# Taps of a causal depthwise convolution: from diagonal float32r products to float32 products of four taps by 32 channels in four column tiles

## The chip, the cores and the metric

The kernel runs as one launch on one core of a Trainium2 chip. The metric is device time in microseconds of that core. A core has TensorE for matrix products (PE in the profile; PEld is its loading of the stationary operand), VectorE (DVE), ScalarE (ACT), GpSimd (POOL) and SyncE (SP). SP here issues every data transfer and computes nothing. PSUM is the memory that TensorE writes, SBUF the working memory of 128 partitions.

## The reference, cut to what matters

The program is two transformer blocks on 512 tokens of width 1024, all in float32. The change lies in one mixer of the second block, a Conformer convolution:

```python
def causal_dwconv(x, w):
    k_w = w.shape[0]
    return lax.conv_general_dilated(
        x, w[:, None, :].astype(x.dtype), window_strides=(1,), padding=[(k_w - 1, 0)],
        dimension_numbers=('NWC', 'WIO', 'NWC'), feature_group_count=x.shape[-1])

def conformer_conv(h, w_in, b_in, dw, dw_b, ln_g, ln_b, w_out, b_out):
    D = h.shape[-1]
    u = h @ w_in + b_in
    u = u[..., :D] * jax.nn.sigmoid(u[..., D:])
    u = causal_dwconv(u, dw) + dw_b
    u = jax.nn.silu(layernorm(u, ln_g, ln_b))
    return u @ w_out + b_out
```

Each of the 1024 channels is convolved over time with its own 31 taps (CONV_WIDTH = 31). There is no product across channels in the taps.

## The kernel before, in words

Data lie with channels on partitions: a tensor of 1024 channels is eight tiles of 128 partitions by 512 tokens, the groups m = 0 to 7. Nearly the whole program is dense matrix products. To keep float32 precision they are split: a value is written as hi + lo in the faster type float32r, and `mm3` (L357 to L361) does three products, hi by lo, lo by hi and hi by hi, on lines 359, 360 and 361. `weights` (L311 to L326) loads a weight block of 128 x 2048 into `raw` by SP (L322), casts it to `whi` on ACT (L323) and subtracts on VectorE, or on the engine `lo_on`, to get `wlo` (L324).

The stage is `conformer`. Its loop has three steps per group:

- `inputs(m)` loads the weights of the group and makes two products of 24 float32r matmuls each, for the gate and the value. The low part of the weights is made on VectorE for groups 0 and 1 and on GpSimd for the rest. Three buffers of whi and wlo take turns; `raw` has two.
- `gated(m)` makes u = (value + bias) * sigmoid(gate + bias) (L1176 sg, L1177 the sigmoid, L1181 t, L1183 u) into one of three padded buffers `ub` with 30 zeros ahead of the 512 tokens. Then it puts some taps on TensorE: u is split into uh (ACT, L1187) and ul (GpSimd, L1188), and for each of these taps ACT writes two 128 x 128 diagonal matrices with the tap's rates (L1193, dgh and dgl), and `mm3` multiplies them with u shifted by the tap. Groups 0 to 4 have 5 such taps, then 6, 10 and 20: 61 in all. ACT brings the sum to SBUF with the bias (L1196).
- `convolved(m)` does the rest. VectorE multiplies and adds one tap after the other (L1204 the first, then L1218, `scalar_tensor_tensor`, 128 x 512), alternating between two accumulators. For groups 0 to 6 six further taps are multiplied on ACT (L1211) and added on GpSimd (L1213). GpSimd adds the parts (L1220, L1222); for group 7 VectorE does (L1224, L1225).
- `summed(m)` subtracts an approximate mean on GpSimd (L1234; the mean comes from group 0 alone, L1232), squares on ACT (L1236) and adds both to running sums over channels by two float32 products with a matrix of 1/1024 (L1238).

The loop is software-pipelined: in turn m come inputs(m + 1), gated(m), summed(m - 2), convolved(m - 1). The order on each engine's queue is fixed when the program is built: a list scheduler simulates the engines and takes the instructions that are ready, the earlier of the program first. Every queue runs in order, SP's too.

After the loop the variance is made from the sums (L1253 to L1255), then the norm, SiLU and the output product follow; these lines do not change.

Elsewhere in the program, the attention of the first block has float32 products whose stationary operand is 64 columns wide and whose output is one half of the 128 PSUM partitions: single ones in `stick_breaking` (L727), and pairs for two heads, issued one behind the other into both halves, in `pair` (L776). The linear-recurrence stage copies between SBUF tiles by SP (L1585, ME<-AR, 64 partitions).

Of the kernel before, what the change touches and what calls it, by code (L numbers as in the profile page):

```python
# [11 lines left out]
F32 = mybir.dt.float32  # L12
F32R = mybir.dt.float32r
# [6 lines left out]
P = 128  # L20
# [65 lines left out]
def host(inp):  # L86
# [64 lines left out]
    vec("conv_dw", b["conv_dw"][0].reshape(31, KT, P).transpose(2, 1, 0).reshape(P, 248))  # L151
# [984 lines left out]
def conformer(k):  # L1136
    nc, tc, c = k.nc, k.tc, k.c
    W, PE_TAPS, POOL_TAPS = 31, (5,) * 5 + (6, 10, 20), (6,) * 7 + (0,)
    with ExitStack() as s1:
        k.psum(s1, 6)  # L1140
        stp = k.pool(s1, name="cf_st", bufs=1, space=PSUM)
# [4 lines left out]
        sums = [stp.tile([P, S], F32, name=f"sum{i}") for i in range(2)]  # L1146
        with ExitStack() as s2:
# [3 lines left out]
            ub = [tp.tile([P, S + W - 1], F32, name=f"ub{i}", bufs=1) for i in range(3)]  # L1151
            for u in ub:
                nc.gpsimd.memset(u[:, 0:W - 1], 0.0)  # L1153
            d = lambda m, j: k.v("conv_dw", m * W + j)
            rate_h = tp.tile([P, KT * W], F32R, name="rate_h", bufs=1)
            rate_l = tp.tile([P, KT * W], F32, name="rate_l", bufs=1)
            o0, _ = k.at["conv_dw"]
            raw = k.vecs[:, o0:o0 + KT * W]
            nc.scalar.copy(rate_h, raw)
            nc.gpsimd.tensor_tensor(rate_l, raw, rate_h.bitcast(F32), op=ALU.subtract)  # L1160
            rates = rate_h.bitcast(F32), rate_l

            def inputs(m):
# [3 lines left out]
                w = k.weights(k.I["conv_in"][m], 256, lo_on=nc.gpsimd if m > 1 else None)  # L1167
# [5 lines left out]
            def gated(m, ps, psv):  # L1173

                sg = tp.tile([P, S], F32, name="sg_t")
# [7 lines left out]
                nc.vector.scalar_tensor_tensor(u[:, W - 1:], t, k.v("conv_b_in", m), sg, op0=ALU.add, op1=ALU.mult)  # L1183
                ps = k.mm.tile([P, S], F32, name="ps")
                n = PE_TAPS[m]
# [9 lines left out]
                if m < KT - 1:  # L1195
                    nc.scalar.activation(conv[m], ps, AF.Identity, bias=k.v("conv_dw_b", m))  # L1196
                return u, ps

            def convolved(m, u, ps):

                o = conv[m]
                n = PE_TAPS[m]
                o2 = tp.tile([P, S], F32, name="conv2")
                nc.vector.tensor_scalar(o2, u[:, n:n + S], d(m, n), None, op0=ALU.mult)  # L1204
                if m == KT - 1:
                    n += 1
                    nc.vector.tensor_scalar(o, u[:, n:n + S], d(m, n), k.v("conv_dw_b", m), op0=ALU.mult, op1=ALU.add)
                o3 = None
                for j in range(W - POOL_TAPS[m], W):
                    t = tp.tile([P, S], F32, name="ct" if o3 else "conv3")  # L1210
                    nc.scalar.activation(t, u[:, j:j + S], AF.Copy, scale=d(m, j))  # L1211
                    if o3:
                        nc.gpsimd.tensor_tensor(o3, o3, t, op=ALU.add)  # L1213
                    else:
                        o3 = t
# [705 lines left out]
```

## Time and profile before

| what | value |
|---|---|
| time, median of 3 runs | 2643.24 us (2641.21 to 2645.35) |
| the profiled execution: time | 2642.88 us |
| its span, first to last instruction | 2641.1 us |
| mean granted TensorE clock | 0.969 |
| busy share of the span | PE 94%, PEld 75%, DVE 62%, ACT 44%, POOL 15% |
| transfers | 249.59 MB, mean 95 GB/s |

The profile is of one execution. Times in it are microseconds from the start of the span, and durations of groups are busy time, mean ns of one. A row of a group names line, engine, operation and tiles as out<-in; what follows the bar is busy time and mean, then the idle time of the engine just before, with what ended it. In the timeline equal instructions that follow each other are merged into one row with their count. Matmuls overlap, and their recorded ends are modelled, so TensorE is better read from start to start. The granted clock is a share of full speed: 1.00 is 2.4 GHz and 0.50 is 1.2 GHz.

### The profile page before, as it was taken

How to read it: one execution, taken by the hardware profiler on the slowest of the kernel's cores; microseconds unless marked ns; L12 is line 12 of the kernel's file. 1: busy time of each engine (PE TensorE's matmuls, PEld its weight loads, DVE VectorE, ACT ScalarE, POOL GpSimd, SP SyncE). 2: the span in 40 equal slices, each digit the busy share in tenths (PEclk: the TensorE clock that was granted, in tenths of full speed). 3: DMA queues.
4: the chain of work that ended last, by engine and by line, in shares of the span. 5: the costliest groups of instructions: out<-in, count | busy, mean ns of one | idle time of the engine just before them, and what ended most of it. 6: DMA issues, size and time to landing. Idle time of an engine off the chain costs nothing.

```text
span 2641.1 us, 32709 instructions
## 1 busy us (share of the span) xinstructions
PE 2471.1 (94%) x13005; PEld 1992.1 (75%) x13005; DVE 1628.8 (62%) x2217; ACT 1161.9 (44%) x1934; POOL 383.3 (15%) x291
## 2 busy tenths in 40 slices
PE   7999999999997999999998999999966798999997
PEld 6777777888886777878777888888744587888886
DVE  5345665543346877776466474646899665665655
ACT  5464544332234455665545342424534543433333
POOL 1001000000002663332010000000576300000000
PEclk9999999999998999999999999999988899999999
DMA  5113334222223544121332222222210031222221
GB/s 171 61 52 103 120 120 158 80 96 98 99 84 125 180 164 146 63 57 49 122 110 80 80 96 96 96 96 81 95 48 16 16 128 49 96 96 96 96 92 68
DMA packets 72837, 249.59 MB, mean 95 GB/s; under 512 B 8296, under 2 KB 19688, under 8 KB 54888
## 3 DMA queue, kind: packets, MB, share of 16 engines
q1 hardware_dynamic: 72684, 247.50, 27.5%
q8 instruction: 102, 1.67, 0.3%
q14 instruction: 51, 0.42, 0.0%
HBM read 217.84 MB, written 25.43 MB: 92 GB/s over the span
## 4 chain that ended last, share of the span: by engine, by line
PE 80%; DVE 12%; ACT 3%; DMA 3%; issue 2%; POOL 1%; SPq 0%; DVEq 0%; ACTq 0%; POOLq 0%
PE ps L359 19%; PE ps L360 19%; PE ps L361 19%; DVE conv L1218 5%; PE pt L1606 3%; PE fl L359 1%; PE fl L360 1%; PE fl L361 1%; PE y L1707 1%; DVE wlo L324 1%; PE pt L1583 1%; ACT whi L323 1%; PE y L1706 1%; PE o L776 1%; PE s L703 1%
## 5 line engine op out<-in xcount | busy, mean ns | idle before, releaser
L323 ACT CAST whi<-raw 128x2048 fp32r<-128x2048 f32 (+4 forms) x251 | 346.1, 1386 | 537.2 <-PE ps L361 439.1
L324 DVE TENSOR_TENSOR wlo<-raw,whi 128x2048 fp32r<-128x2048 f32 (+4 forms) x232 | 384.4, 1661 | 198.2 <-ACT whi L323 194.2
L930 DVE TENSOR_TENSOR x<-ps,x 128x512 f32<-128x512 f32 x94 | 64.1, 690 | 218.8 <-PE ps L361 218.8
L1218 DVE SCALAR_TENSOR_TENSOR conv<-ub,vecs,conv 128x512 f32<-128x512 f32 x136 | 162.5, 1250 | 0.4
L324 POOL TENSOR_TENSOR wlo<-raw,whi 128x2048 fp32r<-128x2048 f32 (+2 forms) x19 | 60.9, 3209 | 632.5 <-ACT whi L323 632.5
L1120 ACT ACTIVATE cv<-u,vecs 128x512 f32<-128x512 f32 x88 | 63.0, 720 | 150.3 <-DVE u L1118 150.1
L1118 DVE TENSOR_TENSOR u<-ps,rms 128x512 f32<-128x512 f32 x88 | 60.3, 688 | 76.1 <-PE ps L361 76.0
L1345 POOL TENSOR_SCALAR mx<-h,vecs 128x512 f32<-128x512 f32 x40 | 80.5, 2017 | 61.5 <-DVE mx6l L351 25.8
L1618 ACT CAST qb<-pt 128x512 bf16<-128x512 f32 x112 | 63.8, 590 | 37.2 <-PE pt L1606 36.3
L1289 POOL TENSOR_TENSOR fo<-x,rms 128x256 f32<-128x256 f32 x6 | 4.9, 843 | 486.1 <-DVE rms L415 486.1
L1121 DVE SCALAR_TENSOR_TENSOR cv<-u,vecs,cv 128x512 f32<-128x512 f32 x88 | 65.7, 748 | 11.2 <-ACT cv L1120 10.9
L359 PE MATMUL ps<-xg0h,wlo 128*128 128x512 f32 x164 | 68.8, 421 | 2.7 <-ACT xg0h L353 1.9
L360 PE MATMUL ps<-xg0l,whi 128*128 128x512 f32 x164 | 65.0, 397 | 3.6 <-DVE xg0l L354 3.6
L1153 POOL MEMSET ub<- 128x30 f32 x3 | 0.3, 123 | 461.5 <-DVE cv L1122 461.5
L1122 DVE SCALAR_TENSOR_TENSOR cv<-u,vecs,cv 128x512 f32<-128x512 f32 x88 | 65.8, 749 | 1.7
L359 PE MATMUL ps<-xg1h,wlo 128*128 128x512 f32 x164 | 65.7, 401 | 0.0
L360 PE MATMUL ps<-xg1l,whi 128*128 128x512 f32 x164 | 65.7, 400 | 0.0
L1625 DVE CAST_PREDICATED Z<-ball,pt 128x512 bf16<-128x512 int16 x80 | 53.1, 683 | 20.2 <-PE pt L1606 19.7
L360 PE MATMUL ps<-xg7l,whi 128*128 128x512 f32 x164 | 64.1, 391 | 1.4 <-DVE xg7l L354 1.4
L361 PE MATMUL ps<-xg1h,whi 128*128 128x512 f32 x164 | 64.9, 396 | 0.0
L361 PE MATMUL ps<-xg0h,whi 128*128 128x512 f32 x164 | 64.7, 394 | 0.0
L359 PE MATMUL ps<-xg2h,wlo 128*128 128x512 f32 x164 | 64.7, 395 | 0.0
(1253 smaller groups left out, 7562.5 us busy)
## 6 DMA issues: line engine op xcount, KB each, us to landing
raw<-ffn_in SPq DMA_DIRECT2D x44, 1024.0 KB, 4.7
raw<-xkv SPq DMA_DIRECT2D x64, 256.0 KB, 2.9
raw<-w_up SPq DMA_DIRECT2D x16, 1024.0 KB, 4.8
raw<-w_down SPq DMA_DIRECT2D x16, 1024.0 KB, 4.8
raw<-ffn_out SPq DMA_DIRECT2D x16, 1024.0 KB, 4.8
rk_scr<-ev SPq DMA_DIRECT2D x48, 256.0 KB, 2.4
raw<-w_in_fm SPq DMA_DIRECT2D x16, 512.0 KB, 4.6
pg<-rk_scr SPq DMA_DIRECT2D x8, 1024.0 KB, 5.7
```

Source lines behind the costliest of these rows:

```text
L323: a = hi_on.tensor_copy(hi[:, m], raw) if hi_on else nc.scalar.copy(hi[:, m], raw)
L324: b = (lo_on or nc.vector).tensor_tensor(lo[:, m], raw, hi[:, m].bitcast(F32), op=ALU.subtract)
L359: nc.tensor.matmul(ps, wl, xh, start=start, stop=False, skip_group_check=skip)
L360: nc.tensor.matmul(ps, wh, xl, start=False, stop=False, skip_group_check=skip)
L361: nc.tensor.matmul(ps, wh, xh, start=False, stop=stop, skip_group_check=skip)
L930: nc.vector.tensor_tensor(k.x[i], ps, k.x[i], op=ALU.add)
L1121: nc.vector.scalar_tensor_tensor(t, u[:, 1:S + 1], d(1), t, op0=ALU.mult, op1=ALU.add)
L1122: nc.vector.scalar_tensor_tensor(t, u[:, 0:S], d(0), t, op0=ALU.mult, op1=ALU.add)
L1218: nc.vector.scalar_tensor_tensor(a, u[:, j:j + S], d(m, j), a, op0=ALU.mult, op1=ALU.add)
L1345: nc.gpsimd.tensor_scalar(t, h[m][:, 0:S], k.v(f"mu{i}", m), None, op0=ALU.mult)
L1606: nc.tensor.matmul(o[:, u], lhs[:, u] if len(lhs.shape) == 3 else lhs, rhs[:, u] if len(rhs.shape) == 3 else rhs, start=True, stop=True)
L1618: nc.scalar.copy(t, o)
```

## The change

The taps 0 to 19 go to TensorE for every group, the other 11 stay with one ACT and ten VectorE operations. For the products, the 128 channels of a group are cut into four blocks g of 32. A tile `ut` of 128 partitions holds, for block g, four copies of its 32 channels one under the other, copy j shifted by j tokens; sixteen transfers by SP make it from u. A block `dg[:, 4s + g]` of 128 x 32 holds at row 32j + i, column i the rate of tap 4s + j of channel i of block g. One float32 product of dg with `ut[:, g]` from token 4s on then adds four taps for 32 channels, and its output is 32 of the 128 PSUM partitions. Five steps s by four blocks g are 20 products a group. dg is made by one VectorE multiplication of a mask with rates from a new input, `conv_taps`, that also carries all the taps and is loaded by one transfer at the start of the stage; the taps leave the common vector table. The low parts of all weights are made on VectorE. The two accumulators become one, the last addition reads PSUM. The running sums become additions on VectorE, with two products after the loop instead of two in each turn.

```diff
+CONV_STEPS = 5
...
+    dw = b["conv_dw"][0]
+    pk = dw[:4 * CONV_STEPS].reshape(CONV_STEPS, 4, KT, 4, 32).transpose(1, 4, 2, 0, 3).reshape(P, -1)
+    a["conv_taps"] = np.concatenate([dw.reshape(31, KT, P).transpose(2, 1, 0).reshape(P, 248), pk,
+                                     np.arange(P)[:, None] % 32 == np.arange(32)[None]], 1)
...
-    W, PE_TAPS, POOL_TAPS = 31, (5,) * 5 + (6, 10, 20), (6,) * 7 + (0,)
+    W, NS = 31, CONV_STEPS
+    L = S + W + 1
...
-        k.psum(s1, 6)
-        stp = k.pool(s1, name="cf_st", bufs=1, space=PSUM)
+        k.psum(s1, 8)
...
+        taps = cp.tile([P, 248 + KT * NS * 4 + 32], F32, name="taps")
+        nc.sync.dma_start(taps, k.I["conv_taps"])
...
-                w = k.weights(k.I["conv_in"][m], 256, lo_on=nc.gpsimd if m > 1 else None)
+                w = k.weights(k.I["conv_in"][m], 256)
...
+                dg = tp.tile([P, NS * 4, 32], F32, name="dg")
+                nc.vector.tensor_tensor(dg, mask.unsqueeze(1).to_broadcast([P, NS * 4, 32]),
+                                        rows[:, m].unsqueeze(2).to_broadcast([P, NS * 4, 32]), op=ALU.mult)
...
-                uh, ul = [tp.tile([P, S + W - 1], F32R, name=nm) for nm in ("uh", "ul")]
-                nc.scalar.copy(uh, u)
-                nc.gpsimd.tensor_tensor(ul, u, uh.bitcast(F32), op=ALU.subtract)
-                for j in range(n):
-                    dg = []
-                    for nm, r in zip(("dgh", "dgl"), rates):
-                        dg.append(tp.tile([P, P], F32R, name=nm, bufs=6))
-                        nc.scalar.activation(dg[-1], c["ident"], AF.Copy, scale=r[:, m * W + j:m * W + j + 1])
-                    k.mm3(ps, *dg, uh[:, j:j + S], ul[:, j:j + S], j == 0, j == n - 1)
+                ut = tp.tile([P, 4, L - 4], F32, name="ut")
+                for j in range(4):
+                    for g in range(4):
+                        nc.sync.dma_start(ut[32 * j:32 * j + 32, g], u[32 * g:32 * g + 32, j:j + L - 4])
+                return u, ut, dg
...
+                for s in range(NS):
+                    for g in range(4):
+                        nc.tensor.matmul(ps[32 * g:32 * g + 32], dg[:, 4 * s + g], ut[:, g, 4 * s:4 * s + S],
+                                         start=s == 0, stop=s == NS - 1, skip_group_check=True)
+                o, n = conv[m], 4 * NS
+                nc.scalar.activation(o, u[:, n:n + S], AF.Identity, scale=rate(m, n), bias=k.v("conv_dw_b", m))
+                for j in range(n + 1, W):
+                    nc.vector.scalar_tensor_tensor(o, u[:, j:j + S], rate(m, j), o, op0=ALU.mult, op1=ALU.add)
+                nc.vector.tensor_tensor(o, ps, o, op=ALU.add)
...
-                nc.gpsimd.tensor_tensor(o, o, mean, op=ALU.subtract)
-                q = tp.tile([P, S], F32, name="csq")
+                nc.vector.tensor_tensor(o, o, mean, op=ALU.subtract)
+                q = tp.tile([P, S], F32, name="csq") if m else total[1]
                 nc.scalar.activation(q, o, AF.Square)
-                for i, r in enumerate((o, q)):
-                    nc.tensor.matmul(sums[i], c["ones_d"], r, start=(m == 0), stop=(m == KT - 1))
+                if m:
+                    nc.vector.tensor_tensor(total[0], conv[0] if m == 1 else total[0], o, op=ALU.add)
+                    nc.vector.tensor_tensor(total[1], total[1], q, op=ALU.add)
...
+            sums = [k.mm.tile([P, S], F32, name="ps") for _ in range(2)]
+            for ps, r in zip(sums, total):
+                nc.tensor.matmul(ps, c["ones_d"], r, start=True, stop=True)
```

## Rows read from the trace of the kernel before

**Rows 1.** The page, part 4: the chain that ended last, by line.

```profile
PE ps L359 19%; PE ps L360 19%; PE ps L361 19%; DVE conv L1218 5%; PE pt L1606 3%; PE fl L359 1%; PE fl L360 1%; PE fl L361 1%; PE y L1707 1%; DVE wlo L324 1%; PE pt L1583 1%; ACT whi L323 1%; PE y L1706 1%; PE o L776 1%; PE s L703 1%
```

**Rows 2.** Busy time by stretch: start of the stage, loop, tail, one input set.

```profile
core 0: us, PE busy (x) PEld busy (x) DVE busy (x) ACT busy (x) POOL busy (x), PEclk, DMA share, GB/s
1858.70:1881.00 22.30, 21.35 (x92) 16.94 (x92) 14.76 (x11) 11.42 (x12) 9.53 (x2) 1.00 0.38 132
1881.00:2070.00 189.00, 137.54 (x506) 102.02 (x504) 187.98 (x169) 90.27 (x188) 125.01 (x66) 0.86 0.10 36
2070.00:2091.00 21.00, 6.44 (x8) 2.51 (x8) 8.64 (x7) 7.54 (x11) 15.34 (x12) 0.64 0.00 0
1900.70:1911.60 10.90, 10.90 (x49) 8.82 (x47) 10.90 (x12) 6.04 (x10) 6.15 (x5) 1.00 0.00 0
```

**Rows 3.** Groups of VectorE in the stage: busy us, mean ns.

```profile
L1218 DVE SCALAR_TENSOR_TENSOR conv<-ub,vecs,conv 128x512 f32<-128x512 f32 x136 | 162.5, 1250 | 0.4
L1204 DVE TENSOR_SCALAR conv<-ub,vecs 128x512 f32<-128x512 f32 x8 | 9.0, 1123 | 0.7 <-POOL conv L1220 0.6
L1183 DVE SCALAR_TENSOR_TENSOR ub<-t,vecs,sg_t 128x512 f32<-128x512 f32 x8 | 7.0, 871 | 0.0
L324 DVE TENSOR_TENSOR wlo<-raw,whi 128x2048 fp32r<-128x2048 f32 x3 | 6.8, 2283 | 0.7 <-ACT whi L323 0.7
L1176 DVE TENSOR_TENSOR sg_t<-ps,rms 128x512 f32<-128x512 f32 x8 | 5.4, 680 | 0.0
L1181 DVE TENSOR_TENSOR t<-ps,rms 128x512 f32<-128x512 f32 x8 | 5.4, 678 | 0.0
...
L1225 DVE TENSOR_TENSOR conv<-ps,conv 128x512 f32<-128x512 f32 x1 | 0.7, 692 | 0.0
```

**Rows 4.** L1218: min/median/max ns; then its timeline where GpSimd idles.

```profile
L1218 DVE SCALAR_TENSOR_TENSOR conv<-ub,vecs,conv x136: 735/745/5105, 1881.6 to 2069.1; 128x512 f32<-128x512 f32 x136
...
2061.71 6.05 DVE L1218 SCALAR_TENSOR_TENSOR conv<-ub,vecs,conv 128x512 f32<-128x512 f32 x9
```

**Rows 5.** Groups of GpSimd in the stage, the first two of six.

```profile
L1213 POOL TENSOR_TENSOR conv<-conv,ct 128x512 f32<-128x512 f32 x35 | 57.1, 1634 | 22.1 <-ACT ct L1211 20.6 <-ACT conv L1211 0.8
L324 POOL TENSOR_TENSOR wlo<-raw,whi 128x2048 fp32r<-128x2048 f32 x6 | 29.7, 4943 | 34.6 <-ACT whi L323 34.6
```

**Rows 6.** Timeline of TensorE: the first product of the stage.

```profile
1858.76 0.39 PE L359 MATMUL ps<-xg0h,wlo 128*128 128x512 f32 x1
```

**Rows 7.** Timeline of all engines behind the last taps.

```profile
2069.74 0.69 DVE L1225 TENSOR_TENSOR conv<-ps,conv 128x512 f32<-128x512 f32 x1
2069.89 1.26 POOL L1220 TENSOR_TENSOR conv<-conv,conv 128x512 f32<-128x512 f32 x1 [11.03 <-DVE conv L1218]
...
2073.89 2.08 PE L1238 MATMUL sum<-conv,call 128*128 128x512 f32 x2 [4.18 <-POOL conv L1234]
...
2079.41 0.60 ACT L1253 ACTIVATE var<-sum 128x512 f32<-128x512 f32 x1 [3.69 <-PE sum L1238]
```

**Rows 8.** Groups of ACT in the stage.

```profile
L323 ACT CAST whi<-raw 128x2048 fp32r<-128x2048 f32 x9 | 17.0, 1898 | 8.1 <-PE ps L361 8.1
L1177 ACT ACTIVATE sg_t<-sg_t,vecs 128x512 f32<-128x512 f32 x8 | 5.8, 723 | 36.8 <-DVE sg_t L1176 36.8
...
L1211 ACT ACTIVATE conv<-ub,vecs 128x512 f32<-128x512 f32 x7 | 5.1, 722 | 11.8 <-POOL conv L1222 11.8
L1236 ACT ACTIVATE csq<-conv 128x512 f32<-128x512 f32 x8 | 5.0, 627 | 13.5 <-POOL conv L1234 13.5
```

**Rows 9.** Timeline of TensorE: one float32 product of 512 columns, and the next.

```profile
313.53 1.02 PE L819 MATMUL s<-ka,qa 66*128 66x512 f32 x2
314.39 0.22 PE L820 MATMUL s<-ball,b_ident 128*128 128x128 bf16 x1
```

**Rows 10.** Timeline of TensorE: one 64-column product, a pair, and what follows each.

```profile
77.46 1.07 PE L727 MATMUL o<-sb_a,V 128*64 128x512 f32 x2
78.46 0.59 PE L703 MATMUL s<-sq,sk 64*128 64x384 f32 x1
...
283.19 1.08 PE L776 MATMUL o<-pts,V 128*64 128x512 f32 x4
284.20 0.59 PE L819 MATMUL s<-ka,qa 66*128 66x384 f32 x1
```

**Rows 11.** SP's queue: issue in ns (min/median/max) and landing in us, copies and loads.

```profile
L1585 SPq DMA_DIRECT2D ME<-AR x32: 461/588/675, 990.2 to 1234.6; - x32
...
DMA to landing us min/median/max: 2.2/2.3/6.5
...
L322 SPq DMA_DIRECT2D raw<-conv_in x8: 327/328/328, 1842.3 to 1915.8; - x8
...
raw<-conv_in SPq DMA_DIRECT2D x8, 1024.0 KB, 4.7
```

More of the change, by code (lines that the diff above doesn't have):

```diff
@@ L150, in host @@
     vec("conv_b_in", fm(b["conv_b_in"][0]))
-    vec("conv_dw", b["conv_dw"][0].reshape(31, KT, P).transpose(2, 1, 0).reshape(P, 248))
+    dw = b["conv_dw"][0]
+    pk = dw[:4 * CONV_STEPS].reshape(CONV_STEPS, 4, KT, 4, 32).transpose(1, 4, 2, 0, 3).reshape(P, -1)
+    a["conv_taps"] = np.concatenate([dw.reshape(31, KT, P).transpose(2, 1, 0).reshape(P, 248), pk,
+                                     np.arange(P)[:, None] % 32 == np.arange(32)[None]], 1)
     for n in ("conv_dw_b", "conv_ln_g", "conv_ln_b", "conv_b_out"):
@@ L1145, in conformer @@
         mean = cp.tile([P, S], F32, name="mean")
-        sums = [stp.tile([P, S], F32, name=f"sum{i}") for i in range(2)]
+        total = [cp.tile([P, S], F32, name=f"total{i}") for i in range(2)]
+        taps = cp.tile([P, 248 + KT * NS * 4 + 32], F32, name="taps")
+        nc.sync.dma_start(taps, k.I["conv_taps"])
+        rate = lambda m, j: taps[:, m * W + j:m * W + j + 1]
+        rows = taps[:, 248:248 + KT * NS * 4].rearrange("p (m n) -> p m n", n=NS * 4)
+        mask = taps[:, 248 + KT * NS * 4:]
         with ExitStack() as s2:
@@ L1150, in conformer @@
             rstd = None
-            ub = [tp.tile([P, S + W - 1], F32, name=f"ub{i}", bufs=1) for i in range(3)]
+            ub = [tp.tile([P, L], F32, name=f"ub{i}", bufs=1) for i in range(3)]
             for u in ub:
                 nc.gpsimd.memset(u[:, 0:W - 1], 0.0)
[L1154 to L1161, printed above, removed]
+                nc.gpsimd.memset(u[:, S + W - 1:], 0.0)
             def inputs(m):
@@ L1182, in gated @@
                 u = ub[m % 3]
-                nc.vector.scalar_tensor_tensor(u[:, W - 1:], t, k.v("conv_b_in", m), sg, op0=ALU.add, op1=ALU.mult)
-                ps = k.mm.tile([P, S], F32, name="ps")
-                n = PE_TAPS[m]
-                uh, ul = [tp.tile([P, S + W - 1], F32R, name=nm) for nm in ("uh", "ul")]
-                nc.scalar.copy(uh, u)
-                nc.gpsimd.tensor_tensor(ul, u, uh.bitcast(F32), op=ALU.subtract)
-                for j in range(n):
-                    dg = []
-                    for nm, r in zip(("dgh", "dgl"), rates):
-                        dg.append(tp.tile([P, P], F32R, name=nm, bufs=6))
-                        nc.scalar.activation(dg[-1], c["ident"], AF.Copy, scale=r[:, m * W + j:m * W + j + 1])
-                    k.mm3(ps, *dg, uh[:, j:j + S], ul[:, j:j + S], j == 0, j == n - 1)
@@ L1195, in gated @@
[L1195 to L1215, printed above, removed]
-                for j in range(n + 1, W - POOL_TAPS[m]):
-                    a = (o2, o)[(j - n) % 2]
-                    nc.vector.scalar_tensor_tensor(a, u[:, j:j + S], d(m, j), a, op0=ALU.mult, op1=ALU.add)
-                if m < KT - 1:
-                    nc.gpsimd.tensor_tensor(o, o, o2, op=ALU.add)
-                    if o3:
-                        nc.gpsimd.tensor_tensor(o, o, o3, op=ALU.add)
-                else:
-                    nc.vector.tensor_tensor(o, o, o2, op=ALU.add)
-                    nc.vector.tensor_tensor(o, ps, o, op=ALU.add)
@@ new lines, in gated, with convolved @@
+                nc.vector.scalar_tensor_tensor(u[:, W - 1:S + W - 1], t, k.v("conv_b_in", m), sg, op0=ALU.add, op1=ALU.mult)
+                ut = tp.tile([P, 4, L - 4], F32, name="ut")
[3 more added lines that the diff above has]
+                return u, ut, dg
+            def convolved(m, u, ut, dg):
+                ps = k.mm.tile([P, S], F32, name="ps")
+                for s in range(NS):
[7 more added lines that the diff above has]
+                nc.vector.tensor_tensor(o, ps, o, op=ALU.add)
```

## Prediction

> **What bounds the kernel now.** I began with the page: TensorE is the end of the chain of waits nearly everywhere, and the one line of another engine with a large share is the vector multiply-add of the convolution, L1218, at 5% [rows 1]. So the stage of the change is not bound like the rest. The table by stretch says so: in 1881 to 2070 us VectorE is busy 187.98 of 189.00 us, TensorE only 137.54 [rows 2], while in the stretch just before TensorE hardly stops. VectorE's groups show why: 136 multiply-adds take 162.5 us, a mean of 1250 ns [rows 3]. The same instruction runs at (6.05 - 0.74) / 8 = 0.66 us from start to start in a stretch where GpSimd is idle [rows 4]; GpSimd's groups (L1213, L324 and four more, each of which reads SBUF) fill 125.01 us of the stretch [rows 2, 5]. I read the slow ones as VectorE held up by GpSimd; both the count and the price of the multiply-adds are then open to the change. The stage runs from its first product at 1858.76 [rows 6] to ACT's read of the sums at 2079.41 [rows 7]: 220.6 us. A group of 128 channels costs VectorE (162.5 + 9.0 + 7.0 + 5.4 + 5.4) / 8 = 23.7 us [rows 3].
>
> **Removed.** 56 of 136 multiply-adds; on TensorE 61 taps of three float32r products; on ACT the diagonals, casts and tap products; all of GpSimd's work in the loop; eight pairs of sums. None of it but the vector work and the closing chain was on the path.
>
> **VectorE after, per group.** Ten multiply-adds 9 x 0.66 + 0.74 = 6.7 [rows 4]; the split of the weights, which moves here from GpSimd for groups 2 to 7, 2.28; sg and t 0.68 each, the last add from PSUM 0.69 [rows 3]; u 0.74, as the same operation undisturbed [rows 4]; the subtraction of the mean and two running totals, 3 x 0.68 by the t row. The diagonal block dg, 128x640 with both inputs broadcast, has no row: between t (512 elements, 0.68) and the split (2048, 2.28), by length 0.81. Sum 14.6 us, provided that GpSimd stays idle; if not, the ten would cost up to 1.7 us each. ACT has the cast 1.90, sigmoid 0.72, one tap 0.72 and square 0.63 [rows 8], 4.0 us, hidden.
>
> **TensorE after, per group.** 48 input products take 10.9 us (the last stretch of [rows 2]). The taps are five rounds of four float32 products of 128 rows by 32 columns, each round over four column tiles. A float32 product of 512 columns costs 314.39 - 313.53 = 0.86 us [rows 9]. Whether four overlap is the question of this change, and the kernel before already answers half of it: one product on a 64-column tile occupies TensorE from 77.46 to 78.46, and a pair on two such tiles with different moving data from 283.19 to 284.20 [rows 10]. The second tile is free. I extend this to four, as it is the nearest row: 5 x 0.86 plus 0.15 for entering and leaving (1.01 - 0.86) = 4.45 us. The upper end is no overlap, 20 x 0.86 = 17.2; below 4.3 nothing is possible, as one tile has five products in a row. Sum 15.35 us a group: TensorE becomes the bound, 0.75 us ahead of VectorE.
>
> **The copies.** Sixteen a group on SP's queue, SBUF to SBUF. The nearest row, ME<-AR, takes 0.59 us to issue and lands 2.3 us after issue; a weight load lands in 4.7 and takes 0.33 to issue [rows 11]. Bounds: 16 x 0.33 + 2.3 = 7.6 and 16 x 0.59 + 2.3 = 11.7 us from u to the last copy. I take 11.7, by the SBUF row. In the middle of the loop two input sets and two tap sets (2 x 10.9 + 2 x 4.45 = 30.7 us) lie between a group's input set and its own taps; u takes some 3 to 10 of them, so the copies are hidden. For the last group it is not. What waits behind the copies on SP is the next weight load: a rival below. The load of the taps is one more transfer on that queue, off the path unless its SBUF is freed late; 0 to 4.7 us, I take 0.
>
> **Sum.** TensorE starts at 1858.8, with 1 us lost at the start as before (21.35 of 22.30 us busy [rows 2]). Eight input sets are 87.2, and seven tap sets 31.2: 1978.2. The last u: input set 7 ends at 1969.3 (five tap sets ahead of it), VectorE's add for group 5 waits for its taps until 1973.7, then sg, sigmoid and u 2.1 [rows 3, 8], the copies: 1987.5. The last tap set is 4.45 at full clock, 8.9 at half; TensorE has then been idle 9 us, and the granted clock was 0.64 in the idle tail before [rows 2], so I take 6.5: 1994. Then add 0.69, subtract 0.68, square 0.63, total 0.68 and one product of about 2 us [rows 7]: 1998.7, against 2079.4. This replaces the tail of 9.7 us in which three GpSimd operations and four double products followed the last add [rows 7]. Gain 80.7 us. Against it I set 8 us for waits between two engines 0.75 us apart: none at best, one split of 2.28 late in each group, 18 us, at worst. Net 72.7: 2642.88 - 72.7 = 2570 us for the profiled execution, which is 0.36 us under the median of the runs; I forecast **2570**. Its own range: 2556 (no waits, short copies, full clock) to 2583 (18 us of waits, half clock).
>
> **Rivals.** (B) *Column tiles overlap only in part*, two at a time: a set is 10 x 0.86 + 0.15 = 8.75 us, input and tap sets end at 2017, the last u's copies delay that to 2022.4, and the sums come at 2027.4: 2591. For it: no row shows four tiles. Against: in the pair the second tile costs 10 ns (1.07 and 1.08 us [rows 10]), no sign of a shared limit.
> The Trainium skill, "TensorE: Matmul & The Clock Gate", section "Part 3: Packing small matmuls", reports 2.38 times for three column tiles and 3.07 times for four row tiles, where full overlap would be 3 and 4; by 3.07 a set would be an estimated 17.2 / 3.07 = 5.6 us and the time some 9 us above my forecast, and the pair in the trace agrees with overlap but not with a loss.
>
> (C) *Column tiles do not overlap in this order.* Each product is two records, and if TensorE starts the next tile only after the second, a set is 17.2 us; all sets end at 1859.8 + 87.2 + 137.6 = 2084.6, the copies are hidden, the sums come at 2089.6, 10 us later than now: 2653, **slower**. It decides from a set of 15.9 us up. The pair speaks against it.
>
> (D) *SP's queue.* Copies wait in order for u, and the load for the group after next may stand behind them. Its weights are then ready u + 9.4 + 4.7 + 1.9 + 2.28 = 18.3 us after u, 20.4 after the input set, and needed after 10.9 + 2 x 4.45 = 19.8; behind ten multiply-adds 6.7 later. Late by 0.6 to 7.3 us in five groups: 4 us each, 2590, at most 2607. For it: program order has the load behind the copies. Against: the loads of before were issued as soon as their buffer was free, ahead of other work.
>
> **How the numbers follow.** Forecast 0.66, B 0.12, D 0.11, C 0.11. About 0.2% (5 us) can be told from no change; C's price is twice that, so a little of it may read as the same: faster 0.88, same 0.02, slower 0.10. The range starts under the forecast's own low end, 2555, and reaches past B and D to 2612, which leaves out C and little else.
>
> **What would show it.** Right: in the profile after, multiply-adds with a mean near 0.74 us, 80 of them; GpSimd without work in the loop; the four tiles' first records a few ns apart and a tap set in about 4.5 us; TensorE dense through the loop at clock 1.00 with one gap before the last set; the sums some 73 us earlier. Wrong: tap sets of 9 or 17 us (B, C); input products that wait for wlo while SP holds copies (D); multiply-adds that stay at 1.2 us with GpSimd idle, which would break my reading of VectorE and add up to 5 us a group.

## The result and the profile after

| kernel | median | runs | ratio to before, 95% interval |
|---|---|---|---|
| before, on the same chip | 2644.3 us | 2641.21 to 2646.2 | |
| after | 2564.01 us | 2561.08 to 2567.13 | 0.9698 [0.9681, 0.9714] |

The change is faster by 80 us, 3.0%. The forecast was 2570 us in a range of 2555 to 2612. The profiled execution of after took 2561.08 us, with a span of 2558.9 us. Line numbers below are those of the changed kernel: L366 to L368 are the three products of `mm3`, L329, L330 and L331 the load of a weight block, its cast and its low part, L1195 the copies, L1203 the tap products, L1208 the multiply-adds, L1209 the addition that reads PSUM, L1241 the read of the sums.

The chain that ended last, by line, the same line of the page as in [rows 1]. The multiply-add, 5% before, is gone from it, and the tap products stand there with 1%:

```profile
PE ps L366 21%; PE ps L367 21%; PE ps L368 20%; PE pt L1594 3%; PE ps L1203 1%; DVE wlo L331 1%; PE y L1695 1%; PE fl L366 1%; DMA raw<-xkv 1%; PE fl L367 1%; ACT whi L330 1%; PE fl L368 1%; PE pt L1571 1%; PE y L1694 1%; PE o L783 1%
```

Busy time by stretch, to be read beside [rows 2]: the start of the stage, the loop, the tail, one turn of the loop, then the gap ahead of the last tap set and that set.

```profile
core 0: us, PE busy (x) PEld busy (x) DVE busy (x) ACT busy (x) POOL busy (x), PEclk, DMA share, GB/s
1855.20:1881.00 25.80, 25.80 (x113) 21.02 (x112) 19.83 (x23) 14.99 (x14) 0.00 (x0) 1.00 0.46 156
1881.00:1970.00 89.00, 89.00 (x474) 56.88 (x474) 80.34 (x109) 20.87 (x23) 0.00 (x0) 1.00 0.49 139
1970.00:1997.60 27.60, 18.90 (x129) 7.49 (x127) 19.45 (x27) 5.07 (x7) 0.00 (x0) 0.87 0.33 88
1909.00:1924.54 15.54, 15.54 (x92) 10.13 (x88) 15.35 (x22) 5.20 (x7) 0.00 (x0) 1.00 0.68 215
...
1979.60:1986.10 6.50, 0.12 (x4) 0.00 (x0) 6.50 (x11) 0.63 (x1) 0.00 (x0) 0.80 0.61 149
1986.10:1993.30 7.20, 7.12 (x40) 3.81 (x40) 1.52 (x3) 0.00 (x0) 0.00 (x0) 0.70 0.09 23
```

The bound has changed hands. In the loop TensorE is busy for all of 89.00 us at clock 1.00, VectorE for 80.34, GpSimd for nothing; before, VectorE filled 187.98 of 189.00 us.

VectorE's groups in the stage, beside [rows 3]:

```profile
L1208 DVE SCALAR_TENSOR_TENSOR conv<-ub,taps,conv 128x512 f32<-128x512 f32 x80 | 58.4, 747 | 2.6 <-ACT conv L1206 1.8
...
L1181 DVE TENSOR_TENSOR dg<-taps 128x640 f32<-128x640 f32 x8 | 6.5, 818 | 1.0 <-DMA taps<-conv_taps 1.0
...
L1209 DVE TENSOR_TENSOR conv<-ps,conv 128x512 f32<-128x512 f32 x8 | 5.5, 687 | 9.2 <-PE ps L1203 9.1
```

136 multiply-adds of 1250 ns have become 80 of 747 ns. VectorE now waits for TensorE's taps, 9.1 us in all (last row): 6.0 of them for the last set, 3.1 for the first.

The timeline of after: the stage's first product, the first tap set, one tap set between two input sets, and the end of the stage on TensorE, its weight loading (PEld), VectorE, SP and ACT, beside [rows 6, 7].

```profile
1855.21 0.39 PE L366 MATMUL ps<-xg0h,wlo 128*128 128x512 f32 x1
...
1888.85 1.04 PE L1203 MATMUL ps<-ut,dg 128*32 128x512 f32 x2
1889.82 0.50 PE L366 MATMUL ps<-xg0h,wlo 128*128 128x512 f32 x1
...
1893.76 4.48 PE L1203 MATMUL ps<-ut,dg 128*32 128x512 f32 x34
...
1907.83 1.02 PE L1216 MATMUL ps<-conv,call 128*128 128x512 f32 x2
...
1924.31 4.50 PE L1203 MATMUL ps<-ut,dg 128*32 128x512 f32 x40
1928.74 0.50 PE L366 MATMUL ps<-xg0h,wlo 128*128 128x512 f32 x1
...
1970.93 8.79 PE L1203 MATMUL ps<-ut,dg 128*32 128x512 f32 x80
...
1971.04 0.69 DVE L1189 TENSOR_TENSOR t<-ps,rms 128x512 f32<-128x512 f32 x1 [0.45 <-PE ps L368]
1971.82 0.75 DVE L1191 SCALAR_TENSOR_TENSOR ub<-t,vecs,sg_t 128x512 f32<-128x512 f32 x1
...
1975.29 0.33 SPq L329 DMA_DIRECT2D raw<-conv_out  x1
1975.72 10.81 SPq L1195 DMA_DIRECT2D ut<-ub  x16
...
1986.18 7.45 PE L1203 MATMUL ps<-ut,dg 128*32 128x512 f32 x40 [6.46 <-DVE conv L1208]
...
1987.35 0.18 PEld L1203 LDWEIGHTS ps<-ut,dg 128*32 128x32 f32 x2 [0.35 <-DMA ut<-ub]
...
1993.67 0.69 DVE L1209 TENSOR_TENSOR conv<-ps,conv 128x512 f32<-128x512 f32 x1 [5.99 <-PE ps L1203]
...
1997.04 0.60 ACT L1241 ACTIVATE var<-ps 128x512 f32<-128x512 f32 x1 [1.22 <-PE ps L1237]
```

A product is two records, so a set of 20 is x40. From start to start a tap set takes 1928.74 - 1924.31 = 4.43 us. At the end of the loop the sets of groups 5 and 6 run back to back (x80), then TensorE has nothing until the last set at 1986.18. The row names VectorE as what it waited for, but that multiply-add is no input of the products; the last copies are, and they were issued until 1986.5 (1975.72 + 10.81). The set's first products, one of each block, started one by one as the copies of their block landed, the fourth 1.8 us after the first (the PEld row shows the third waiting for a copy).

The first turn is longer than the others, 19.9 us from set 0 at 1888.85 to set 1 at 1908.78. Two things fill most of the extra 4.4 us: input products stand between the first tap products of set 0, three of which so ran alone, 0.97 us each (1889.82 - 1888.85), and the product for the mean of group 0 (L1216) takes 0.95 us.

From the first product to ACT's read of the sums the stage takes 1997.04 - 1855.21 = 141.8 us, against 220.6 before: 78.8 us of the gain. What follows it is as long as before to within 0.6 us (2561.08 - 1997.04 = 564.0; 2642.88 - 2079.41 = 563.5). This stage began 3.55 us earlier than before, but that is no gain of the change: in the traces of the runs below, none of which touches an earlier stage, it begins anywhere between 1854.5 and 1863.1. The length of the stage is steadier than the time of the run: 141.8 and 142.2 us in the two traces of the change, whose times are 2561.08 and 2566.08.

### The profile page after: what moved, and what is told of

It reads as the page before. It is cut to its first block, busy times and chain, and to the rows that moved or that the text cites. A ratio compares the mean times of both kernels' runs of the same rounds, so it can differ in the third digit from the quotient of the medians.

```text
span 2558.9 us, 32838 instructions
## 1 busy us (share of the span) xinstructions
PE 2437.7 (95%) x13114; PEld 1954.6 (76%) x13114; DVE 1544.6 (60%) x2194; ACT 1096.5 (43%) x1762; POOL 244.5 (10%) x222
## 4 chain that ended last, share of the span: by engine, by line
PE 87%; DVE 5%; DMA 3%; ACT 3%; issue 2%; POOL 0%; SPq 0%; DVEq 0%; ACTq 0%; POOLq 0%
PE ps L366 21%; PE ps L367 21%; PE ps L368 20%; PE pt L1594 3%; PE ps L1203 1%; DVE wlo L331 1%; PE y L1695 1%; PE fl L366 1%; DMA raw<-xkv 1%; PE fl L367 1%; ACT whi L330 1%; PE fl L368 1%; PE pt L1571 1%; PE y L1694 1%; PE o L783 1%
## 5 line engine op out<-in xcount | busy, mean ns | idle before, releaser
L330 ACT CAST whi<-raw 128x2048 fp32r<-128x2048 f32 (+4 forms) x251 | 346.4, 1386 | 567.1 <-PE ps L368 450.8
L331 DVE TENSOR_TENSOR wlo<-raw,whi 128x2048 fp32r<-128x2048 f32 (+4 forms) x238 | 396.7, 1672 | 197.1 <-ACT whi L330 193.0
L331 POOL TENSOR_TENSOR wlo<-raw,whi 128x512 fp32r<-128x512 f32 (+2 forms) x13 | 32.1, 2477 | 600.9 <-ACT whi L330 600.9
L366 PE MATMUL ps<-xg0h,wlo 128*128 128x512 f32 x164 | 68.3, 419 | 0.0
L367 PE MATMUL ps<-xg6l,whi 128*128 128x512 f32 x164 | 64.0, 390 | 1.1 <-DVE xg6l L361 1.1
L368 PE MATMUL ps<-xg0h,whi 128*128 128x512 f32 x164 | 64.3, 392 | 0.0
L366 PE MATMUL ps<-xg1h,wlo 128*128 128x512 f32 x164 | 64.2, 392 | 0.0
L368 PE MATMUL ps<-xg1h,whi 128*128 128x512 f32 x164 | 64.2, 392 | 0.0
L366 PE MATMUL ps<-xg2h,wlo 128*128 128x512 f32 x164 | 64.1, 392 | 0.0
L368 PE MATMUL ps<-xg7h,whi 128*128 128x512 f32 x164 | 64.0, 390 | 0.0
L368 PE MATMUL ps<-xg3h,whi 128*128 128x512 f32 x164 | 64.0, 390 | 0.0
```

The costliest lines, as they stand in the source:

```text
L330: a = hi_on.tensor_copy(hi[:, m], raw) if hi_on else nc.scalar.copy(hi[:, m], raw)
L331: b = (lo_on or nc.vector).tensor_tensor(lo[:, m], raw, hi[:, m].bitcast(F32), op=ALU.subtract)
L366: nc.tensor.matmul(ps, wl, xh, start=start, stop=False, skip_group_check=skip)
L367: nc.tensor.matmul(ps, wh, xl, start=False, stop=False, skip_group_check=skip)
L368: nc.tensor.matmul(ps, wh, xh, start=False, stop=stop, skip_group_check=skip)
```

## The experiments

All of them edit the convolution alone; three of them also touch what follows the stage, by a subtraction moved to VectorE or a load of output weights moved on SP's queue. "Stage" is the length just defined, read from the trace of each run; it tells differences of 1 or 2 us apart that the time, with intervals of some 4 us either way, does not.

| run | time | ratio to before, 95% interval | stage |
|---|---|---|---|
| after | 2564.01 | 0.9698 [0.9681, 0.9714] | 141.8 |
| after, run again | 2564.85 | 0.9699 [0.9685, 0.9714] | 142.2 |
| tap products tile by tile | 2613.98 | one run | 188.8 |
| GpSimd kept busy | 2580.07 | one run | 160.1 |
| before, GpSimd idle | 2611.06 | 0.9876 [0.986, 0.9893] | 187.8 |
| 16 taps on TensorE | 2572.0 | 0.9728 [0.9713, 0.9742] | 149.3 |
| 24 taps on TensorE | 2570.74 | 0.9724 [0.971, 0.9739] | 147.9 |
| all copies on two queues | 2576.99 | 0.9749 [0.9732, 0.9765] | 156.0 |
| the same, with a subtraction on VectorE | 2578.34 | 0.9751 [0.9733, 0.977] | 155.9 |
| load behind the last copies | 2564.56 | 0.9706 [0.9692, 0.9721] | 143.5 |
| last copies shared, load behind them | 2563.16 | 0.9701 [0.9686, 0.9715] | 138.8 |
| last copies mostly on ACT | 2562.63 | 0.9702 [0.9686, 0.9718] | 142.7 |
| third ut buffer, last copies shared | 2561.13 | 0.9685 [0.9671, 0.9699] | 139.7 |

The change run again, unedited, shows what repeats: the turn of 15.54 us, the gap of 7 us, the stage to within 0.4 us, and a start of the stage 4 us later.

> The kernel after once more, beside the next three on one chip: 2564, as measured, ratio 0.970 to the kernel before.

**Is it the column tiles?** The same 20 products, ordered tile by tile in place of round by round:

```diff
-                for s in range(NS):
-                    for g in range(4):
+                for g in range(4):
+                    for s in range(NS):
```

> The 20 tap products of a group in the order of the tiles: the five of tile 0, then the five of tile 1, and so on, in place of four tiles in turn. Theory (the gain rests on products of different tiles that stand next to each other in TensorE's queue): within a tile nothing overlaps, so a set takes 20 x 0.86 = 17.2 us, or 14.6 where the last product of a tile overlaps with the first of the next; the loop's turn goes from 15.5 to 25.5 to 28 us, 10 us of the gap ahead of the last set are hidden, and the time is 2635 to 2655. Rival (each tile has its own queue, so the order does not matter): 2564, sets of 3.9 us from first to last start.

Measured: 2613.98 us, 50 us over the change. A set in the timeline of this run, and a turn of its loop in the table by stretch (columns as above):

```profile
1941.94 12.29 PE L1203 MATMUL ps<-ut,dg 128*32 128x512 f32 x40
```

```profile
1930.00:1953.30 23.30, 23.30 (x90) 12.17 (x88) 15.72 (x19) 4.07 (x4) 0.00 (x0) 1.00 0.34 94
```

The set takes 12.3 us instead of 4.5, a turn 23.3 instead of 15.5. So the overlap is real, and it hangs on the order in TensorE's queue. It is not lost altogether: four tiles of five products each at 0.86 us would take 17.2 us without overlap [rows 9]. By the sum, each change of tile saves (17.2 - 12.3) / 3 = 1.6 us, about two products: the next tile starts early only beside the last two of the tile before. The records agree: six start in the first 2.60 us of the set, three products of one tile, and ten in the next 2.60. My expectation took it for nearly none, and so lay 21 us too high even at its lower end.

**Is it the idle GpSimd?** Six additions of 128x512 on GpSimd in each turn, whose results nobody reads:

```diff
+                spare = tp.tile([P, S], F32, name="spare", bufs=1)
+                for j in range(6):
+                    nc.gpsimd.tensor_tensor(spare, u[:, j:j + S], u[:, j + 1:j + 1 + S], op=ALU.add)
```

> The kernel after with six additions of 128x512 on GpSimd in each turn, into a tile that nobody reads. Theory (GpSimd reading SBUF holds VectorE's two-input operations up): six multiply-adds of a group go from 0.66 to about 1.7 us, their mean from 747 to some 1350 ns, VectorE's turn from 14.6 to 20.9 us and past TensorE's 15.5; time 2564 + 8 x 5.4 = 2607. Rival (the slow multiply-adds of before came from their own chain or from ACT's reads of the same tile): mean 750 ns, 2564.

Measured: 2580.07 us. Its groups of VectorE and GpSimd in the stage:

```profile
L1211 DVE SCALAR_TENSOR_TENSOR conv<-ub,taps,conv 128x512 f32<-128x512 f32 x80 | 80.9, 1027 | 2.6 <-ACT conv L1206 1.8
L1221 DVE TENSOR_TENSOR conv<-conv,mean 128x512 f32<-128x512 f32 x8 | 8.8, 1103 | 0.0
...
L1189 DVE TENSOR_TENSOR t<-ps,rms 128x512 f32<-128x512 f32 x8 | 5.5, 681 | 0.0
...
L1209 POOL TENSOR_TENSOR spare<-ub 128x512 f32<-128x512 f32 x48 | 73.8, 1537 | 99.6 <-DVE ub L1191 96.3
```

With GpSimd reading SBUF for 73.8 us, the multiply-adds go from 747 to 1027 ns and the subtraction, with both inputs in SBUF, from 686 to 1103; t, which reads PSUM, does not change. This is the mechanism that the prediction read from [rows 3, 4]. The price, 16 us, is far below the expected 43. VectorE's extra work is 80.9 - 58.4 = 22.5 us of multiply-adds and a few of the rest; and TensorE kept its turns of 15.5 us to the end of the loop, where the lag showed at once: set 6 began at 1987.0 and set 7 at 2006.07.

**How much does idle GpSimd bring by itself?** The kernel before, with all that GpSimd did in the loop put on VectorE, the six taps of each group that went to ACT and GpSimd included:

```diff
-    W, PE_TAPS, POOL_TAPS = 31, (5,) * 5 + (6, 10, 20), (6,) * 7 + (0,)
+    W, PE_TAPS, POOL_TAPS = 31, (5,) * 5 + (6, 10, 20), (0,) * 8
...
-                w = k.weights(k.I["conv_in"][m], 256, lo_on=nc.gpsimd if m > 1 else None)
+                w = k.weights(k.I["conv_in"][m], 256)
...
-                nc.gpsimd.tensor_tensor(ul, u, uh.bitcast(F32), op=ALU.subtract)
+                nc.vector.tensor_tensor(ul, u, uh.bitcast(F32), op=ALU.subtract)
```

> The kernel before with GpSimd's work in the loop moved to VectorE (low parts of u and of the weights, final addition, subtraction of the mean) and GpSimd's six taps a group given to VectorE as multiply-adds: GpSimd idle, without any column tiles. Theory: VectorE's turn is 25 x 0.66 + 0.5 + splits 2.28 + 0.68 + five operations of 0.68 to 0.74 = 23.6 us in groups 0 to 4, 175 us in all eight against 189: time some 2627, so the idle GpSimd alone is worth about 15 of 80 us and the taps on TensorE the rest. Rival (the slow multiply-adds do not come from GpSimd): they keep a mean near 1250 ns and the time rises above 2700.

Measured: 2611.06 us, 33 us under the kernel before, with 42 more multiply-adds on VectorE. Its group of them, and the start of its stage, its loop and its tail by stretch:

```profile
L1218 DVE SCALAR_TENSOR_TENSOR conv<-ub,vecs,conv 128x512 f32<-128x512 f32 x178 | 121.5, 741 | 0.1
```

```profile
1856.95:1881.00 24.05, 24.05 (x105) 19.53 (x104) 17.66 (x20) 13.22 (x13) 0.00 (x0) 1.00 0.37 136
1881.00:2030.00 149.00, 124.34 (x488) 94.36 (x486) 147.30 (x214) 64.37 (x143) 0.00 (x0) 0.91 0.12 43
2030.00:2045.40 15.40, 9.96 (x12) 3.65 (x12) 11.90 (x19) 2.55 (x5) 0.00 (x0) 0.56 0.00 1
```

VectorE is still the bound (147.30 of 149.00 us), at 741 ns an operation. In [rows 5] GpSimd spent 57.1 us on 35 additions; here those taps cost VectorE 42 x 0.68 = 29 us (121.5 / 178 for one) and the other 136 cost 70 us less than before. At the end of the stage it is 4.1 us from the last addition, at 2040.65, to ACT's read of the sums, at 2044.74, against 9.7 before [rows 7]. So of the 80 us some 33 are to be had by giving GpSimd nothing to do, nearly 6 of them behind the last addition; the other 47 come with the rest of the change, the tap products on TensorE above all, and no run here splits them. My expectation was 16 us too high, but its sum of VectorE's work held: 175 us expected, 176.9 busy in the three stretches. It was set against the 189 us of the loop alone: with the start of the stage VectorE's work of before is 202.7 us (14.76 + 187.98 [rows 2]), and the shorter end was not counted.

**Is twenty the right number of taps?** `CONV_STEPS` at 4 and at 6:

```diff
-CONV_STEPS = 5
+CONV_STEPS = 4
```

```diff
-CONV_STEPS = 5
+CONV_STEPS = 6
```

> Four steps in place of five: 16 taps on TensorE, 14 multiply-adds on VectorE. Theory (TensorE is the bound, VectorE less than 1 us behind it): TensorE's turn falls by 0.86 to 14.7, VectorE's rises by 2.65 to 17.3 and becomes the bound; 8 x 1.8 = 14 us more: 2577. Rival (VectorE still has room, because its work fills gaps): 8 x 0.86 less, 2557.

> Six steps in place of five: 24 taps on TensorE, six multiply-adds on VectorE. Theory (TensorE is the bound in every turn): its turn rises by 0.86 to 16.4 us, eight turns cost 7 us more: 2571, whatever VectorE saves (2.65 a turn). Rival (VectorE is late in each turn and TensorE waits for it): 2564 or less.

Measured: 2572.0 and 2570.74 us, 8 and 7 us over the change. With 24 taps the turn is 16.4 us, 0.9 longer, and seven of those are the 6 us of its stage (147.9 - 141.8). With 16 taps TensorE's turn falls to 14.7 us, yet the stage is 7.5 us longer; its table by stretch shows why:

```profile
1900.00:1970.00 70.00, 70.00 (x366) 47.66 (x364) 67.34 (x97) 16.82 (x18) 0.00 (x0) 1.00 0.50 139
1970.00:1990.00 20.00, 9.18 (x71) 2.52 (x70) 19.83 (x29) 3.35 (x3) 0.00 (x0) 0.77 0.55 164
1990.00:2008.00 18.00, 6.59 (x33) 3.43 (x30) 15.83 (x25) 2.31 (x4) 0.00 (x0) 0.69 0.00 1
```

TensorE is dense until it runs out of work, and VectorE, now the slower, is behind by then and finishes alone. So of 16, 20 and 24 taps, 20 is where the two engines are nearest to balance, as the 0.75 us between them in the prediction says.

**Why the gap ahead of the last set?** Two misses came first. I held SP's issue of sixteen copies for the cause, and shared all groups' copies between SP and ACT:

```diff
-                        nc.sync.dma_start(ut[32 * j:32 * j + 32, g], u[32 * g:32 * g + 32, j:j + L - 4])
+                        (nc.sync, nc.scalar)[g % 2].dma_start(ut[32 * j:32 * j + 32, g], u[32 * g:32 * g + 32, j:j + L - 4])
```

> Half of the sixteen copies of a group issued on ACT's queue, half on SP's. Theory (the issue time of the copies, and a weight load that waits ahead of them on SP's queue, keep TensorE idle for 7 us ahead of the last set, at whose end its clock is low): the last copy lands 4 to 5 us earlier, the last set starts earlier and runs faster: 4 to 8 us less, 2556 to 2560; the loop's turns stay at 15.5 us. Rival (the copies are bound by their transport, not by their issue): 2564.

Measured: 2576.99 us, 13 us slower than the change. The waits of ACT in this run (total, times, longest), then TensorE's timeline:

```profile
ACT csq L1220 <- DMA ut<-ub: 36.6, 5, 8.3
ACT conv L1206 <- DVE ub L1191: 18.0, 2, 12.1
```

```profile
1906.90 0.39 PE L368 MATMUL ps<-xg7h,whi 128*128 128x512 f32 x1
1923.69 2.07 PE L1216 MATMUL ps<-conv,call 128*128 128x512 f32 x2 [16.40 <-DVE conv L1209]
```

ACT's queue runs in order, and its copies stood ahead of group 0's tap and squares and held them. The mean product of group 0 (L1216) waited for that group in TensorE's own order, 1923.69 - 1906.90 = 16.8 us. The gap ahead of the last set did shrink, to 2.5 us, but by much less than this cost. With the subtraction behind the loop moved from GpSimd to VectorE as well the time stayed so:

```diff
-            nc.gpsimd.tensor_tensor(conv[m], conv[m], mean, op=ALU.subtract)
+            nc.vector.tensor_tensor(conv[m], conv[m], mean, op=ALU.subtract)
```

> The same, and behind the loop the subtraction of the mean ahead of the norm on VectorE in place of GpSimd. Theory (GpSimd's subtractions, 1.6 us each, set the pace there and hold VectorE's multiplications up to 1.8 us): first product of the output block 2 us earlier, each of the eight parts 0.3 us faster, so 3 to 4 us under the run with two queues. Rival (ACT's SiLU and casts set the pace): no difference to it.

Measured: 2578.34 us, no gain in the time. The trace does show one, behind the stage: the first output product followed ACT's read of the sums by 11.0 instead of 11.7 us, and from that read to the end of the span it is 560.1 us (2574.2 - 2014.12), against 561.9 in the run before it and in after, and 561.6 or more in every other trace. So in this one trace 1.8 of the expected 3 to 4 us came; the start of the stage, 3.7 us later than in the run before it, hides them in the time.

Next I took the load on SP for the cause. It stands between the last u and the first copy in the timeline of after (1975.29), so I queued it behind the copies; and in a second run I also shared the last group's copies alone, by `(nc.scalar if g % 2 == 0 and m == KT - 1 else nc.sync)`. In a third the load stayed and ACT took twelve of the last sixteen (`g < 3`).

```diff
-            self.last_load = nc.sync.dma_start(raw, src[:, m])
+            with self.tc.issue_after(self.hold.pop().ins) if len(self.hold) == 1 else ExitStack():
+                self.last_load = nc.sync.dma_start(raw, src[:, m])
...
+        k.hold = [k.copy, None]
```

> The change, with one edit: the second load of the output weights, which stood on SP ahead of the last group's copies and waited there for its buffer, is queued behind them. My theory (SP's order made the first copy of the last group wait from 1972.57 to 1975.72): the copies start and land 3.1 us sooner, the gap ahead of the last tap set falls from 7 to about 4 us, and the time is about 2561 us, 3 us under the change; the output weights arrive at about 1987 and are needed after 2008. Rival (the copies are late because of u, or the delayed load costs as much at the first output product): 2564 us or more.

> As the run before, and the last group's sixteen copies are shared, eight on SP's queue and eight on ACT's; all other groups stay on SP. My theory (the loss with all groups on two queues came from ACT's in-order queue early in the loop, not from the sharing): the last copies land at about 1972.6 + 8 x 0.6 + 2 = 1979.4 us, when TensorE ends the tap sets ahead; no gap, last set at 4.5 to 5.5 us, so about 8 us under the change: 2556 us. Rival (copies on ACT's queue cost wherever they stand, as ACT's squares and the last sums queue behind them): 2564 us or more.

> The change, with twelve of the last group's sixteen copies on ACT's queue and four on SP's, where the load of the output weights stays ahead of them. My theory: ACT issues its twelve from about 1973.5 on in 7.2 us, landing at 1982.7, SP its four from 1975.7 to 1978.1; the gap falls from 7 to 3 us and the time is about 2560 us. Rival as before: 2564 us or more.

Measured: 2564.56, 2563.16 and 2562.63 us; none is told apart from the change. By the length of the stage the second is 3.1 us shorter, the other two are 1.6 and 0.9 longer. The first run's timeline of TensorE, SP and VectorE at the end of the loop shows that the load alone was not what held the copies:

```profile
1973.08 5.36 PE L1209 MATMUL ps<-ut,dg 128*32 128x512 f32 x48
...
1973.97 0.75 DVE L1196 SCALAR_TENSOR_TENSOR ub<-t,vecs,sg_t 128x512 f32<-128x512 f32 x1
...
1977.64 10.01 SPq L1200 DMA_DIRECT2D ut<-ub  x16
...
1994.77 2.29 DVE L336 TENSOR_TENSOR wlo<-raw,whi 128x2048 fp32r<-128x2048 f32 x1 [6.66 <-ACT whi L335]
1996.98 0.68 DVE L1215 TENSOR_TENSOR conv<-ps,conv 128x512 f32<-128x512 f32 x1
```

With no load ahead of them the copies still left 2.9 us after u (1973.97 + 0.75 to 1977.64). They left as the tap set of group 5 ended, 1973.08 + 4.43 = 1977.5, and the same holds in the other runs with two `ut` buffers, on ACT's queue too: group 7's copies overwrite the buffer that set 5 reads. In after both waits ended together, the load's at 1975.29 and the buffer's at 1970.93 + 4.43 = 1975.36, so either alone would have held them. The load moved behind them also came back as a cost: its split (2.29 us) now stood ahead of the last addition on VectorE. In the run with the last copies mostly on ACT, ACT needed 11.86 us for its twelve copies and SP 6.78 for its four, where 0.6 us each would be 7.2 and 2.4; a load of 1 MB had been issued just ahead of them, at 1975.92.

The last run gave `ut` a third buffer, and shared the last copies ten to six with the loads where they had been in the program:

```diff
-                ut = tp.tile([P, 4, L - 4], F32, name="ut")
+                ut = tp.tile([P, 4, L - 4], F32, name="ut", bufs=3)
...
-                        nc.sync.dma_start(ut[32
+                        (nc.scalar if m == KT - 1 and (4 * j + g) % 8 < 5 else nc.sync).dma_start(ut[32
```

> The change with a third buffer for ut, and ten of the last group's sixteen copies on ACT's queue, six on SP's; the loads of the output weights stay where they were. The runs with the load behind the copies and with shared copies left 2.9 us between the last u and the first copy, on either queue, and the first copy then went out as the tap set of group 5 ended, whose ut it overwrites. New theory: the two ut buffers, not SP's order, held the last copies. Then ACT's copies go out within 1 us of u and land some 8 us after it; the gap ahead of the last set falls from 7 to about 1 to 2 us, the set takes 5.3, and then VectorE is the limit: the last group's ACT tap is queued behind ten copies (6 us), and its ten multiply-adds (7 us) end about when the last set does. Sums 5 to 6 us sooner in the stage, 2558 us. Rival (something else holds the copies): they still go out 2.9 us behind u, and the time is 2563 us or more.

Measured: 2561.13 us. Its timeline at the same place:

```profile
1978.83 8.79 PE L1203 MATMUL ps<-ut,dg 128*32 128x512 f32 x80
...
1979.72 0.75 DVE L1191 SCALAR_TENSOR_TENSOR ub<-t,vecs,sg_t 128x512 f32<-128x512 f32 x1
...
1980.51 6.64 ACTq L1195 DMA_DIRECT2D ut<-ub  x10
...
1980.54 3.72 SPq L1195 DMA_DIRECT2D ut<-ub  x6
1984.36 0.54 SPq L329 DMA_DIRECT2D raw<-conv_out  x1
...
1991.50 7.83 DVE L1208 SCALAR_TENSOR_TENSOR conv<-ub,taps,conv 128x512 f32<-128x512 f32 x10
...
1991.62 6.54 PE L1203 MATMUL ps<-ut,dg 128*32 128x512 f32 x40 [4.00 <-DVE total L1223]
1999.44 0.69 DVE L1209 TENSOR_TENSOR conv<-ps,conv 128x512 f32<-128x512 f32 x1
```

The copies now leave 0.04 us after u (1980.47 to 1980.51): the third buffer was what they lacked. ACT's ten show it: in the run with the last copies mostly on ACT, with two buffers and no load ahead on ACT's queue, ACT's copies left 2.93 us after u (1973.20 to 1976.13). On SP two things differ, as the scheduler put the load behind the six copies here (1984.36). The gain was not what I expected. The set still starts only at 1991.62, 4 us after the sets ahead of it. ACT's last copy was issued by 1987.15, and the slowest copy of this run landed 6.0 us after issue, against 2.1 in the median; a load of 1 MB goes out from 1984.36 on beside them. Two rows tell what a load just ahead does to the last group's copies, the first of after, the second of the run with the load behind them:

```profile
DMA to landing us min/median/max: 2.0/3.1/5.6
```

```profile
DMA to landing us min/median/max: 2.0/2.0/2.1
```

So a load does delay copies, and in the run with the last copies mostly on ACT, with a load ahead, the row says 2.0/4.4/7.2; that it is what held this set is argued, not tested by itself. VectorE's last ten multiply-adds, which waited for ACT's tap behind ten copies, end at 1999.3, so a sooner set would have gained nothing more. The stage is 2.1 us shorter than in after. The time is 3 us lower than after's and the intervals of the two overlap: no version tried here is shown to beat the change.

## Why the prediction was right

By its own steps; times of the forecast stage are counted from its start at 1858.8, those of after from 1855.2.

- **VectorE was held up by GpSimd.** Right. Forecast 0.74 us for a multiply-add alone, measured 0.747; 1.03 again when GpSimd was given work. GpSimd without work is worth 33 of the 80 us, nearly 6 of them behind the last addition. The 1.7 us that the prediction set as the price beside a busy GpSimd stands in no row; the means are 1.25 before and 1.03 in the run with GpSimd busy.
- **VectorE's turn, 14.6 us.** Right. It is busy 80.34 of 89.00 us of the loop, 14.0 us of a turn of 15.54 (the one turn in the table, with 22 operations against a mean of 19, has 15.35). The diagonal block, which had no row, took 818 ns; the interpolation said 0.81 us. ACT's tap took 816 ns rather than 0.72.
- **A tap set, 4.45 us.** Right: 4.43 from start to start, and the window of 1924.30 to 1924.42 holds four of its records, the first of each tile. This was the step most in doubt, since the rows showed two column tiles and never four. The fourth tile is as free as the second. The Trainium skill, "TensorE: Matmul & The Clock Gate", section "Part 3: Packing small matmuls", has 3.07 times for four row tiles; here four column tiles give 17.2 / 4.43 = 3.9 times, so the loss that the prediction worked out from that figure does not appear. Rival B asked for 8.75 us and is out.
- **Rival C, no overlap and slower than before.** Out for this order of products. That the order can matter was the right thing to ask: with the tiles one after the other a set takes 12.3 us, though not 17.2, and nothing in the sum of the work would tell the two orders apart. Even so it is faster than before, as the set would have to reach 15.9.
- **Rival D, loads behind copies on SP.** Out in the loop: 89.00 of 89.00 us busy on TensorE. SP did wait for u and for buffers, and the weights still came in time.
- **TensorE becomes the bound, 15.35 us a turn.** Right for every turn but the first: 15.54, the first 19.9. The forecast had neither the product for the mean of group 0 nor input products between the first taps. So input set 7 ended at 115.7 us of the stage (1970.93 - 1855.21) where the forecast had 110.5 (1969.3 - 1858.8). A change of the tap number to either side cost 7 or 8 us.
- **The copies are hidden except for the last group.** Right, but two errors cancel on the way, which is luck. The last u was ready at 117.4 us of the stage (1972.57 - 1855.21), forecast 117.0 (1975.8 - 1858.8). Input set 7 ended 5.2 us late; but VectorE made t and u right behind it (1971.04, 1971.82), ahead of the addition for group 5, for whose taps the forecast let it wait 4.4 us. Then a cause was left out: the copies do not start at u but 3.1 us later, when set 5 gives back the second `ut` buffer and the load ahead of them on SP is issued. The prediction had looked at loads behind the copies and not at the one ahead, nor at the buffers of the tile that the copies write. Their issue took 10.8 us for sixteen, where the 0.59 us each of [rows 11] make 9.4; the rest lies between the copies. The last set started at 131.0 us of the stage, forecast 128.7 (1987.5 - 1858.8).
- **The last set, 6.5 us.** 7.45 at a granted clock of 0.70, after 6.5 us in which TensorE did nothing. The clock need not be all of it: its first four products started over 1.8 us, as their copies landed. In the run with the last copies shared, the gap was 2 us and the set took 5.3 us at 1.00, still 0.9 more than a set in the loop.
- **The sums.** Forecast at 139.9 us of the stage without the allowance (1998.7 - 1858.8), measured 141.8.
- **The allowance of 8 us for waits.** This is the term that was mis-sized. The sum without it missed by 1.9 us, so the 8 were 6 too many. The 1.9 are made of larger errors that nearly cancel: input set 7 came 5.2 us late, u followed it 4.9 us sooner than forecast (1.64 against 6.5), the copies started 3.1 us late, from their start to the set it was 1.2 us less than the 11.7, the set took 0.95 more, and from its end to ACT's read it was 3.4 us against 4.7. What the allowance was meant for, two engines 0.75 us apart, cost 0.19 us a turn (15.54 against 15.35). The runs with a slower VectorE show why so little: TensorE kept its turn in each of them, and the lag was paid once, at the end of the loop. With 1.9 in place of 8 the sum gives 2564.1 us, the measured median; that it meets it so closely is chance, as the sum is one for the profiled execution, which took 2561.08 and began the stage 3.55 us early.

## What to carry to other kernels

Before you pack narrow products into column tiles, put them in the queue so that neighbours lie on different tiles: round by round the set took a quarter of what its products take singly, tile by tile seven tenths. When work leaves GpSimd, count what each operation of VectorE with two SBUF inputs gains besides what is removed. When a copy comes late, look for the buffer that it overwrites as well as at what stands ahead of it on its queue, and don't move it to the queue of a computing engine without asking which work then stands behind it.

## What the runs showed that was not expected

- Tile by tile, a column tile's products overlap with the next tile's only by about two products: 1.6 us per change of tile, a set of 12.3 us.
- A slower VectorE did not slow TensorE's loop in any run (turns of 15.5 us with GpSimd busy, 14.7 with 16 taps); its lag appeared whole in the tail.
- The start of the stage, which no edit touched, moved between 1854.5 and 1863.1 us from one execution to the next, more than most edits to its tail were worth. Comparing the stage's length shows what the whole time hides.
- Copies issued just behind a load of 1 MB landed up to 5.6 us after issue, the same copies with the load moved behind them at most 2.1.
- Input products between tap products of one round take the overlap away: three that stood so in the first set ran alone, 0.97 us each.
